# Coefficients of the next pair ahead of the high half of the weight three chunks on, in the output phase of a PEER block

## The chip, the cores and the metric

The kernel runs on one core of a Trainium2 chip. The metric is the device time of one execution in microseconds (us); several executions of one build are given by their median. A core has a matrix engine (TensorE, PE in the profile, with its weight loads as PEld), VectorE (DVE), ScalarE (ACT), GpSimd (POOL) and SyncE (SP). Each engine works through its own queue of instructions in order. Here SyncE issues the large transfers and GpSimd the gathers.

## What is computed

One layer of a streaming encoder for 512 tokens of width 1024: a mixer (a gated convolution beside a gated recurrence), and then PEER, a retrieval over 16384 single-neuron experts. Only PEER matters here:

```python
best_s, best_pos = lax.top_k(cand_s, PEER_TOPK)      # 8 heads, 16 of 16384 experts each
idx = jnp.take_along_axis(cand_i, best_pos, axis=-1)
g = jax.nn.softmax(best_s, axis=-1)
u_sel = expert_u[idx]
act = jax.nn.gelu(jnp.einsum('phkd,pd->phk', u_sel, xb), approximate=False)
coef = (g * act.astype(jnp.float32)).astype(xb.dtype)
return jnp.einsum('phk,phkd->pd', coef, expert_v[idx])
```

All arrays are float32.

## The kernel before

**Two ways for PEER.** The first 128 tokens, and some of the work for 64 more, go the sparse way: GpSimd gathers the chosen rows of `u` and later of `v` (`gath`, L747), and VectorE does one step of some 1.2 us for each gathered tile of 128 rows: a dot product (`dots`, L764) or a weighted sum (`sums`, L780). The other tokens go the dense way: TensorE multiplies with all experts, 128 of them in a chunk, and zero gates remove those that were not chosen.

**Chunks and jobs.** There are 128 `u` chunks (activations, line L87 to L89) and 128 `v` chunks (outputs, L1017). `jobs` (L797) lists them: 124 `u` chunks, then `v` and `u` alternately until the `u` chunks are done, then `v` alone. The first loop (L951, k below `CE` = 124) does the `u` chunks and the searches, the second (L1034) is the output phase.

**The weight's way.** Chunk k's weight is 512 KB. `w_load` (L806) has SyncE load it into `wraw` (4 buffers); `w_high` (L812) has ScalarE copy it to `whi`, rounded to the matrix engine's float32r (L73, 4 buffers); `w_low` (L816) has VectorE subtract, which leaves the rest in `wlo` (L78, 4 buffers). TensorE multiplies with both, so `whi` and `wlo` come free when TensorE is through with the chunk, and `wraw` when ScalarE and VectorE have read it. In round k the kernel asks for the load of chunk k+5, the high half of k+3 and the low half of k+2.

**The coefficients.** For a pair q of `v` chunks (2q and 2q+1), the coefficients are activations times gates. `v_gated(q)` (L896) has ScalarE copy 64 columns of the gates into `cf` (L901), VectorE multiply the other 640 (L903), and ScalarE round `cf` to `ch` (L907). `v_rest(q)` (L910) has VectorE subtract to get `cl` (L914). `cf` has one buffer, `ch` and `cl` two. A `v` chunk is 18 matmuls: for each of 3 token blocks two with `ch` and `whi`, two with `ch` and `wlo`, two with `cl` and `whi`. The first that needs `cl` is the fifth.

**The order around the change.** Both loops are written under a manual schedule: every engine gets its instructions in the order of the program text. A round of the output phase with an even `v` chunk n = 2q puts `w_high(k+3)` first, then `w_low(k+2)`, the gate loads (`v_gates`, L873, SyncE), the reload of spilled activations (`v_act`, L889, SyncE), `v_gated(q+1)`, the 18 matmuls, and a share of the sparse steps, one to three of them (L1058). An odd round has `v_rest(q+1)` in place of `v_gated`. `u_evict` (L833) is ScalarE's pass over a finished `u` chunk; the first matmuls of the output phase reuse the PSUM banks that it frees. The last two rounds of the first loop (k = 122 and 123) hold `v_gated(0)` and `v_rest(0)` for the first pair.

Of the kernel before, what the change touches and what calls it, by code (L numbers as in the profile page):

```python
# [34 lines left out]
def block_kernel(ctx, tc, xT, small, w_ada1, w_ada, b_ada, w_in, w_r, w_i, w_out, w_q, keys, uT, u, v, final_g, out):  # L35
# [35 lines left out]
    def high(raw):  # L71
        hi = wring.tile([128, KB, 128], FR, name="whi", bufs=WB)
        nc.scalar.activation(hi, raw, AF.Copy)  # L73
        return hi
# [10 lines left out]
    def mm3(ps, hi, lo, xh, xl, ks, first, last):  # L85
        for k in ks:
            nc.tensor.matmul(ps, hi[:, k, :], xh(k), start=first and k == ks[0], stop=False)  # L87
            nc.tensor.matmul(ps, hi[:, k, :], xl(k), start=False, stop=False)  # L88
            nc.tensor.matmul(ps, lo[:, k, :], xh(k), start=False, stop=last and k == ks[-1])  # L89
# [657 lines left out]
    def gath(table, idxs, k, key):  # L747
        if key not in rows:
            r = row_tile()
            nc.gpsimd.indirect_dma_start(out=r[:, :], out_offset=None, in_=table,  # L750
                                         in_offset=bass.IndirectOffsetOnAxis(ap=idxs[:, k:k + 1], axis=0))
            rows[key] = r
# [53 lines left out]
    def w_load(k):  # L806
        if k < len(jobs):
            kind, i = jobs[k]
            wraw[k] = load_w(uT[i] if kind == "u" else
                             v[vorder[i] * 128:(vorder[i] + 1) * 128, :].rearrange("p (k e) -> p k e", k=KB))  # L810

    def w_high(k):  # L812
        if k < len(jobs):
            whi[k] = high(wraw[k])

    def w_low(k):  # L816
        if k < len(jobs):
            wlo[k] = low(wraw.pop(k), whi[k])

    def weights(k):  # L820
        w_load(k + 5)
        w_low(k + 2)
# [4 lines left out]
    def spill(q):  # L827
        nc.sync.dma_start(Ad[q], act[q].rearrange("p c t -> p (c t)"))
        act[q] = None
# [3 lines left out]
    def u_evict():  # L833
        if unread:
            c, ps = unread.pop()
            if c % 2 == 0:
                act[c // 2] = ring.tile([128, 2, NU], F32, name="act", bufs=RB // 2)
            nc.scalar.activation(act[c // 2][:, c % 2], ps, AF.Gelu)  # L838

    def u_chunk(k, pool):  # L840
        c = jobs[k][1]
        ps = pool.tile([128, NU], F32, name="ps_act", bufs=2)
        mm3(ps, whi.pop(k), wlo.pop(k), hd, ld, range(KB), True, True)
        u_evict()
        unread.append((c, ps))
        q = c // 2 - RB // 2 + 2
        if c % 2 == 0 and 0 <= q < v0 // 2:
            spill(q)
        pe[0] += 3530
        dve[0] += 1140  # L850
        ac[0] += 1400
# [21 lines left out]
    def v_gates(n):  # L873
        if n >= NE or n in gdone:
            return
        gdone.add(n)
        cc = vorder[n]
        if n < 16 and n % 8 == 0:
            gt = gt8[:, n // 8]
            for t in (2, 3, 1):  # L880
                nc.sync.dma_start(gt[:, 8 * t - 8:8 * t], Gd[t][:, :, cc:cc + 8, :].rearrange("g j i t -> j g i t"))
            for k in range(0, 8, 2):
                gbuf[n + k] = gt[:, :, k:k + 2, :]
        for t in range(1, NT):
            m = n + (4 - t if n < 16 else 13 - 3 * t)
            if m >= 16 and m % 16 == 0 and m < NE:
                load_g16(m, t)

    def v_act(q):  # L889
        if q < NE // 2:  # L890
            c = vorder[2 * q] // 2
            if act[c] is None:
                act[c] = ring.tile([128, 2, NU], F32, name="act", bufs=RB // 2)
                nc.sync.dma_start(act[c].rearrange("p c t -> p (c t)"), Ad[c])
# [15 lines left out]
    def v_rest(q):  # L910
        if q < NE // 2:
            cf, ch = coef[q]
            cl = vp.tile([128, 2, ND], FR, name="cl", bufs=2)
            nc.vector.tensor_sub(cl, cf, ch.bitcast(F32))  # L914
            coef[q] = (ch, cl)
# [10 lines left out]
    def turn(k):  # L926

        awake = [g for g in "gsrd" if g in gens and asleep[g] <= k]
        if gopen and "g" in gens:
            gt = 96 * (k + 1 - gopen[0]) / (KD - KG - gopen[0])  # L930
            if "g" in awake and given["g"] < gt and ac[0] < pe[0] + AD:
                return "g"
            if "s" in awake and (given["g"] < gt and ac[0] < pe[0] + AD or given["s"] < NS * (k - gopen[0]) / (KD - gopen[0])):
                return "s"
        elif "s" in awake:
            return "s"
        elif "r" in awake and ("d" not in awake or given["d"] >= DS * (k - first[0])):
            return "r"
        for g in "dsg" if ac[0] < pe[0] + AD else "ds":
            if g in awake:  # L940
                return g
# [9 lines left out]
    for k in range(CE):  # L951
        weights(k)
        u_chunk(k, psE)
        cur[0] = k
        if sready and not first:
            first.append(k + 4)
            asleep["d"] = k + 4
            for m in range(GB_E - 1):
                gath(u, usteps[m][0], usteps[m][3], m)
        ac[0] = max(ac[0], pe[0] - LEAD)  # L960
        dve[0] = max(dve[0], RHO * pe[0] - LEAD - (HEAD if k < 9 else 0))
        xd = 0
        while dve[0] < RHO * pe[0] or k == KD:
            g = turn(k)
            if k == KD:
                g = next((g for g in "sg" if g in gens), None)
                if "s" not in gens and len(bdone) < XB:
                    g = "d"
            if g is None or (g == "d" and "g" not in gens and xd >= XD):
                break  # L970
            n = next(gens[g], 0)
            if n == 0:
                assert g != "d"
                late_k[g] = k
                del gens[g]
                continue
            if n is None:
                asleep[g] = k + 1
                continue
            dve[0] += n  # L980
            xd += g == "d"
            if gopen or g == "d":
                given[g] += 1 if g in "gd" else n
        w_high(k + 3)
        if k == KD:
            ep.close()
            vp = ctx.enter_context(tc.tile_pool(name="vp", bufs=2, reuse_waits="tile"))
            gp = ctx.enter_context(tc.tile_pool(name="gp", bufs=1, reuse_waits="tile"))
            late[:] = [gp, taken[0] + 10]
            gt8 = vp.tile([128, 2, NG, 8, 16], F32, name="gt", bufs=1)  # L990
        m = k - CE + XE
        if 0 <= m < XE:
            for n in [0] if m < 2 else range(5) if m == XE - 1 else [8]:
                v_gates(n)
        if m >= XE - 2:
            (v_gated, v_rest)[m - XE + 2](0)
    u_evict()
    psx.close()

# [12 lines left out]
    def v_chunk(n, b):  # L1012
        hi, lo, ch, cl = vsp[n]
        bs = slice(b * 128, (b + 1) * 128)
        for st, mv, first, last in ((ch, hi, n == 0, False), (ch, lo, False, False), (cl, hi, False, n == NE - 1)):
            for e in range(2):
                nc.tensor.matmul(accs[b][e], st[:, bs], mv[:, e * 512:(e + 1) * 512], start=first, stop=last)  # L1017
# [15 lines left out]
    steps, done = len(usteps) - len(bdone) + 128, 0  # L1033
    for k in range(CE, len(jobs)):  # L1034
        w_load(k + 5)
        w_high(k + 3)
        w_low(k + 2)
        kind, n = jobs[k]
        if kind == "u":
            u_chunk(k, psP)  # L1040
        else:
            q, e = divmod(n, 2)
            v_gates(n + 5)
            if e == 0:
                v_act(q + 4)
                v_gated(q + 1)
            else:
                v_rest(q + 1)
            vsp[n] = [w.pop(k).rearrange("p k e -> p (k e)") for w in (whi, wlo)] + [c[:, e] for c in coef[q]]
            if n < NE - VT:  # L1050
                for b in range(3):
                    v_chunk(n, b)
                del vsp[n]
            u_evict()
            pe[0] += 4090
            dve[0] += 2005
        if kind == "v":
            share = min((n + 1) / (NE - VE), 1) * (steps + 0.31 * (NE - RB)) - 0.31 * max(n + 1 - RB, 0)  # L1058
            while done < share and next(sparse, None):
                done += 1  # L1060
# [53 lines left out]
CE = 124  # L1114
# [56 lines left out]
```

## Time and profile before

| | |
|---|---|
| median of 3 runs | 1396.99 us (1394.65 to 1399.21) |
| profiled execution | 1397.99 us, of which the span is 1396.2 us |
| TensorE busy | 1343.5 us, 96% |
| VectorE busy | 1243.7 us, 89% |
| ScalarE busy | 757.2 us, 54% |
| GpSimd busy | 531.2 us, 38% |
| transfers | 440.07 MB, mean 315 GB/s; 413 to 414 GB/s from 1100 to 1250 us |
| output phase | first `v` matmul at 831.6 us, last of its loop at about 1371 us |

The profile is of one execution. Its views are: busy time by engine in stretches of the span (with the granted TensorE clock as a fraction), groups of instructions, who waited for whom, and the timeline of one engine. In a timeline row the columns are start in us, duration in us, engine, line of the kernel, operation, result and operands, shapes and count; a bracket at the end gives the idle time ahead of the row and what ended it. Successive rows overlap a little, since an instruction's recorded duration includes the tail of its writes.

### The profile page before, as it was taken

The page shows a single profiled execution, that of the slowest core. Times are in us where ns is not written, and L with a number is a line of the kernel's source. Part 1 is how long each engine was busy: PE and PEld are TensorE (multiplying, and loading weights), DVE is VectorE, ACT ScalarE, POOL GpSimd, SP SyncE. Part 2 cuts the span into 40 slices and gives each one's busy share as a digit, 9 for nine tenths or more (in the row PEclk, how much of TensorE's full clock was granted, in tenths as well). Part 3 has the DMA queues.
Part 4 walks back from the last instruction along what each step waited for, and adds up shares of the span by engine and source line. Part 5 has one row for each costly group of instructions (what it writes and reads, how often), then busy time and mean ns, then how long its engine had stood idle before and what let it go on. Part 6 is the DMA issues. An engine that isn't in the chain of part 4 may idle for free.

```text
span 1396.2 us, 21690 instructions
## 1 busy us (share of the span) xinstructions
PE 1343.5 (96%) x7571; PEld 1167.7 (84%) x7571; DVE 1243.7 (89%) x2452; ACT 757.2 (54%) x1237; POOL 531.2 (38%) x334
## 2 busy tenths in 40 slices
PE   5999998999999999999999989999999999999996
PEld 2566786789999999999999988877778888888885
DVE  6687766899999999999999967898989898898998
ACT  3576634435598699856995434333333433343443
POOL 0000000000245244414342435666756676665660
PEclk9999998999999999999999999999999999999998
DMA  8676332234789999979999999999999999999994
GB/s 350 236 279 210 126 100 81 76 93 143 242 312 387 316 352 373 384 217 347 355 372 340 329 388 376 385 372 414 401 414 409 415 411 415 413 415 412 407 364 178
DMA packets 146929, 440.07 MB, mean 315 GB/s; under 512 B 14722, under 2 KB 42370, under 8 KB 144772
## 3 DMA queue, kind: packets, MB, share of 16 engines
q1 hardware_dynamic: 99812, 267.75, 52.0%
q0 software_dynamic: 46720, 169.89, 31.6%
q8 instruction: 59, 0.97, 0.3%
q10 hardware_dynamic: 288, 1.05, 0.2%
q14 instruction: 50, 0.41, 0.1%
HBM read 393.54 MB, written 45.09 MB: 314 GB/s over the span
## 4 chain that ended last, share of the span: by engine, by line
PE 66%; DVE 15%; DMA 8%; issue 6%; ACT 4%; DVEq 0%; SPq 0%; ACTq 0%
PE acc L1017 26%; PE ps_act L87 7%; PE ps_act L88 7%; PE ps_act L89 7%; DMA wraw<-in_v_dram 6%; PE ps_gt L642 4%; PE ps_z L89 4%; PE ps_z L88 4%; PE ps_z L87 4%; DVE wlo L78 3%; DVE scr L771 3%; DMA rows<-in_u_dram,idx_s 1%; DVE igh L636 1%; ACT whi L73 1%; DVE jh L626 1%
## 5 line engine op out<-in xcount | busy, mean ns | idle before, releaser
L73 ACT ACTIVATE whi<-wraw 128x1024 fp32r<-128x1024 f32 x292 | 308.6, 1057 | 377.6 <-DMA wraw<-in_v_dram 148.4
L78 DVE TENSOR_TENSOR wlo<-wraw,whi 128x1024 fp32r<-128x1024 f32 x292 | 355.6, 1219 | 67.5 <-ACT whi L73 59.5
L87 PE MATMUL ps_act<-h,whi 128*128 128x320 f32 x1024 | 322.4, 315 | 1.6 <-ACT sc L515 1.2
L88 PE MATMUL ps_act<-h,whi 128*128 128x320 f32 x1024 | 317.1, 310 | 0.0
L89 PE MATMUL ps_act<-h,wlo 128*128 128x320 f32 x1024 | 316.9, 309 | 0.0
L750 POOL DMA_INDIRECT rows<-in_u_dram,idx_s x128 | 202.3, 1580 | 225.8 <-DVE scr L771 185.2
L750 POOL DMA_INDIRECT rows<-in_v_dram,idx_s x128 | 226.0, 1766 | 117.7 <-DVE ys L787 90.4
L1017 PE MATMUL acc<-whi,ch 128*128 128x512 f32 x750 | 233.1, 392 | 7.6 <-ACT act L838 4.7
L1017 PE MATMUL acc<-whi,cl 128*128 128x512 f32 x750 | 233.2, 392 | 4.2 <-DVE cl L914 4.2
L1017 PE MATMUL acc<-wlo,ch 128*128 128x512 f32 x750 | 232.2, 391 | 0.0
L87 PEld LDWEIGHTS ps_act<-h,whi 128*128 128x128 f32 x1024 | 193.1, 189 | 2.2 <-ACT sc L515 1.4
L88 PEld LDWEIGHTS ps_act<-h,whi 128*128 128x128 f32 x1024 | 193.0, 189 | 0.2
L89 PEld LDWEIGHTS ps_act<-h,wlo 128*128 128x128 f32 x1024 | 192.8, 188 | 0.0
L750 POOL DMA_INDIRECT rows<-in_u_dram,idx_b x64 | 97.8, 1528 | 213.4 <-DVE scr L771 111.6
L1017 PEld LDWEIGHTS acc<-whi,ch 128*128 128x128 f32 x750 | 141.4, 189 | 38.3 <-ACT act L838 5.5
L1017 PEld LDWEIGHTS acc<-whi,cl 128*128 128x128 f32 x750 | 140.7, 189 | 36.8 <-DVE cl L914 7.7
L1017 PEld LDWEIGHTS acc<-wlo,ch 128*128 128x128 f32 x750 | 141.6, 189 | 29.6
L771 DVE SCALAR_TENSOR_TENSOR scr<-rows,h2n 128x1024 f16<-128x1024 f32 x128 | 156.2, 1220 | 9.8 <-DMA rows<-in_u_dram,idx_s 8.3
L787 DVE SCALAR_TENSOR_TENSOR ys<-rows,acts,ys 128x1024 f32<-128x1024 f32 x127 | 162.6, 1280 | 1.6
L838 ACT ACTIVATE act<-ps_act 128x320 f32<-128x320 f32 x128 | 55.5, 433 | 99.4 <-PE ps_act L89 95.4
L427 POOL DMA_DIRECT2D x1d<-xn x8 | 4.6, 570 | 270.2 <-ACT xn L426 270.2
L642 PE MATMUL ps_gt<-igh,jh 128*128 128x128 f32 x768 | 97.3, 275 | 2.8 <-DVE igh L636 1.3
(269 smaller groups left out, 1896.8 us busy)
## 6 DMA issues: line engine op xcount, KB each, us to landing
wraw<-in_uT_dram SPq DMA_DIRECT2D x128, 512.0 KB
wraw<-in_v_dram SPq DMA_DIRECT2D x128, 512.0 KB
Gd<-stg SPq DMA_DIRECT2D x46, 512.0 KB
wada<-in_w_ada_dram SPq DMA_DIRECT2D x16, 1024.0 KB
Ad<-act SPq DMA_DIRECT2D x48, 320.0 KB
act<-Ad SPq DMA_DIRECT2D x48, 320.0 KB
h<-Gd SPq DMA_DIRECT2D x12, 1024.0 KB
wraw<-in_w_in_dram SPq DMA_DIRECT2D x20, 512.0 KB
```

The costliest lines, as they stand in the source:

```text
L73: nc.scalar.activation(hi, raw, AF.Copy)
L78: nc.vector.tensor_sub(lo, raw, hi.bitcast(F32))
L87: nc.tensor.matmul(ps, hi[:, k, :], xh(k), start=first and k == ks[0], stop=False)
L88: nc.tensor.matmul(ps, hi[:, k, :], xl(k), start=False, stop=False)
L89: nc.tensor.matmul(ps, lo[:, k, :], xh(k), start=False, stop=last and k == ks[-1])
L626: nc.vector.tensor_tensor(jh, iota[:, None, :].to_broadcast([128, 4, 128]), sl[:, 1, t0:t0 + 4, None].to_broadcast([128, 4, 128]), op=OP.i ...
L642: nc.tensor.matmul(pg[:, :, k], jh[:, k, :], ig[:, k, :], start=True, stop=True)
L750: nc.gpsimd.indirect_dma_start(out=r[:, :], out_offset=None, in_=table, in_offset=bass.IndirectOffsetOnAxis(ap=idxs[:, k:k + 1], axis=0))
L771: nc.vector.scalar_tensor_tensor(scr, rows.pop(n), 1.0, hn, op0=OP.mult, op1=OP.mult, accum_out=dst[:, k:k + 1])
L787: nc.vector.scalar_tensor_tensor(ys, rows.pop(k), acts[:, k:k + 1], ys, op0=OP.mult, op1=OP.add)
L838: nc.scalar.activation(act[c // 2][:, c % 2], ps, AF.Gelu)
L1017: nc.tensor.matmul(accs[b][e], st[:, bs], mv[:, e * 512:(e + 1) * 512], start=first, stop=last)
```

## The change

In the rounds k = 122 and 123 of the first loop, and in each `v` round of the output phase, the call of `w_high(k + 3)` is moved behind the call of `v_gated` or `v_rest`. In a `u` round it stays ahead of the chunk's matmuls, now behind `w_low(k + 2)`.

```diff
@@ -981,7 +981,8 @@
             xd += g == "d"
             if gopen or g == "d":
                 given[g] += 1 if g in "gd" else n
-        w_high(k + 3)
+        if k < CE - 2:
+            w_high(k + 3)
         if k == KD:
             ep.close()
             vp = ctx.enter_context(tc.tile_pool(name="vp", bufs=2, reuse_waits="tile"))
@@ -994,6 +995,7 @@
                 v_gates(n)
         if m >= XE - 2:
             (v_gated, v_rest)[m - XE + 2](0)
+            w_high(k + 3)
     u_evict()
     psx.close()
 
@@ -1033,10 +1035,10 @@
     steps, done = len(usteps) - len(bdone) + 128, 0
     for k in range(CE, len(jobs)):
         w_load(k + 5)
-        w_high(k + 3)
         w_low(k + 2)
         kind, n = jobs[k]
         if kind == "u":
+            w_high(k + 3)
             u_chunk(k, psP)
         else:
             q, e = divmod(n, 2)
@@ -1046,6 +1048,7 @@
                 v_gated(q + 1)
             else:
                 v_rest(q + 1)
+            w_high(k + 3)
             vsp[n] = [w.pop(k).rearrange("p k e -> p (k e)") for w in (whi, wlo)] + [c[:, e] for c in coef[q]]
             if n < NE - VT:
                 for b in range(3):
```

## The prediction

> **What bounds the kernel now.** I read the page first. TensorE is the busiest engine, so I went to busy time by stretches, and then to the waits of two stretches of the output phase.
>
> ```profile
> span 1396.2 us, 21690 instructions
> 1050.00:1100.00 50.00, 50.00 (x222) 41.38 (x222) 45.93 (x45) 18.30 (x23) 31.11 (x19) 1.00 1.04 410
> ```
>
> From about 1050 to 1350 us TensorE has no gap (50.00 of 50.00). 222 matmuls in 50 us are 0.225 us each, 4.05 us for a chunk of 18 and 8.11 us for a pair. VectorE has 45.93 us of work in the same 50, and the transfer engines are full (share 1.04, 410 GB/s). So three resources stand close together, and whoever has to wait longer soon shows.
>
> ```profile
> ACT whi L73 <- PE acc L1017: 94.7, 41, 3.0
> ...
> ACT whi L73 <- DMA wraw<-in_v_dram: 76.4, 31, 7.5
> DVE wlo L78 <- ACT whi L73: 16.1, 5, 4.8
> ```
>
> These are the waits of 1050 to 1350 us (total, times, longest). TensorE is not among the waiting. ScalarE waits for a buffer or for the weight to land; VectorE's wait for the high half is 16.1 us in 5 events, each at a late weight. That is all the slack that VectorE has in 300 us.
>
> From 820 to 1050 us TensorE does wait, and these are the waits that the change could touch:
>
> ```profile
> ACT whi L73 <- DMA wraw<-in_v_dram: 72.0, 26, 8.3
> ...
> PEld acc L1017 <- DVE cl L914: 7.7, 9, 1.9
> PEld acc L1017 <- ACT act L838: 5.5, 2, 4.1
> ```
>
> **The change part by part.** Nothing is added or taken away. `w_high` is one ScalarE instruction, and only ScalarE's order changes: VectorE has no instruction of `w_high`, and `v_rest` none on ScalarE. SyncE's and GpSimd's orders stay. What is left is 64 places where ScalarE now does `cf` and `ch` of the next pair ahead of `whi` of chunk k+3. So `ch` no longer stands behind a weight that has not landed; in exchange `whi` stands behind VectorE's `cf` multiply, for which `ch` waits. Behind `whi`, VectorE's `wlo` of k+3 waits, and behind that in VectorE's queue stands `cl` of the very same pair.
>
> *The start of the phase.* Rows of VectorE, ScalarE and the weight loads:
>
> ```profile
> 827.45 0.82 DVE L903 TENSOR_TENSOR cf<-act,gt 128x640 f32<-128x640 f32 x1 [4.86 <-DMA gt<-Gd]
> 830.22 1.23 DVE L78 TENSOR_TENSOR wlo<-wraw,whi 128x1024 fp32r<-128x1024 f32 x1 [1.94 <-ACT whi L73]
> ```
> ```profile
> 829.13 1.06 ACT L73 ACTIVATE whi<-wraw 128x1024 fp32r<-128x1024 f32 x1 [7.87 <-DMA wraw<-in_uT_dram]
> ...
> 830.42 0.84 ACT L907 ACTIVATE ch<-cf 128x768 fp32r<-128x768 f32 x1
> 831.17 0.42 ACT L838 ACTIVATE act<-ps_act 128x320 f32<-128x320 f32 x1
> 831.90 1.06 ACT L73 ACTIVATE whi<-wraw 128x1024 fp32r<-128x1024 f32 x1 [0.31 <-DMA wraw<-in_v_dram]
> ```
> ```profile
> 831.64 0.29 PEld L1017 LDWEIGHTS acc<-whi,ch 128*128 128x128 f32 x1 [4.08 <-ACT act L838]
> 833.33 0.29 PEld L1017 LDWEIGHTS acc<-whi,ch 128*128 128x128 f32 x1 [1.41 <-ACT act L838]
> ```
>
> Now `cf` and `ch` fit into ScalarE's wait for the weight, and the eviction at 831.17 moves to about 830.1: TensorE's first wait shrinks from 4.08 to 3.0 us. But the second eviction stands behind the `whi` at 831.90, which waits for its own weight as before. TensorE reaches that point 1.07 us earlier and waits 1.07 us longer. Term: 0. If that weight were not late, 1.07 us would be gained.
>
> *The price of the new order in a steady pair.* VectorE rows, then ScalarE rows, of one pair:
>
> ```profile
> 1319.39 0.82 DVE L903 TENSOR_TENSOR cf<-act,h 128x640 f32<-128x640 f32 x1
> ...
> 1321.32 1.22 DVE L78 TENSOR_TENSOR wlo<-wraw,whi 128x1024 fp32r<-128x1024 f32 x1
> 1322.46 0.95 DVE L914 TENSOR_TENSOR cl<-cf,ch 128x768 fp32r<-128x768 f32 x1
> ...
> 1326.97 0.81 DVE L903 TENSOR_TENSOR cf<-act,h 128x640 f32<-128x640 f32 x1
> ```
> ```profile
> 1317.93 1.06 ACT L73 ACTIVATE whi<-wraw 128x1024 fp32r<-128x1024 f32 x1 [3.01 <-PE acc L1017]
> ...
> 1320.30 0.85 ACT L907 ACTIVATE ch<-cf 128x768 fp32r<-128x768 f32 x1 [1.11 <-DVE cf L903]
> ```
>
> From `cf`'s start to `ch`'s start are 0.91 us (1319.39 to 1320.30), from `ch` to ScalarE's next instruction 0.75 (830.42 to 831.17), from `whi` to the `wlo` that waits for it 1.09 (829.13 to 830.22). So in the new order `wlo` of k+3 starts no earlier than 2.75 us after `cf`. In this pair one sparse step stands between, and before `wlo` came 1.93 us after `cf`: VectorE would idle for 0.82 us. With two steps between, the cover holds:
>
> ```profile
> 1365.05 0.82 DVE L903 TENSOR_TENSOR cf<-act,h 128x640 f32<-128x640 f32 x1
> ...
> 1368.30 1.22 DVE L78 TENSOR_TENSOR wlo<-wraw,whi 128x1024 fp32r<-128x1024 f32 x1
> ```
>
> 3.25 us against 2.75: nothing, as long as TensorE or the weight doesn't hold `whi` up. In VectorE's timeline 26 of the 64 pairs have one step there. The first of them is
>
> ```profile
> 873.04 0.82 DVE L903 TENSOR_TENSOR cf<-act,gt 128x640 f32<-128x640 f32 x1
> ```
>
> and the last the one at 1326.97 above. Three are before 1000 us, 8 from 1006 to 1064, 8 from 1138 to 1195, 7 from 1276 to 1327. In such a pair VectorE's round grows from 7.58 us (1319.39 to 1326.97) to 8.40, beyond TensorE's 8.11: instead of gaining 0.53 us it loses 0.29. Between 1050 and 1350 there are 17 of them, 13.9 us, against the 16.1 us that VectorE waited there anyway: it just fits, if the late weights land when they did. VectorE's lead covers a run: TensorE starts the chunks of this pair some 8.11 us after 1317.93, at 1326.0, and wants `cl` after four matmuls, at 1326.9; `cl` is done at 1323.4. A lead of 3.5 us against 8 x 0.29 = 2.3 for a run. After a late weight the lead is smaller, so I put 0.2 us a run, 0.6 in all (my estimate; 0 if the lead always holds, 2.3 a run if there is none).
>
> *Where TensorE waits for coefficients.* The two `ch` waits look like the gain:
>
> ```profile
> 969.44 0.30 PEld L1017 LDWEIGHTS acc<-whi,ch 128*128 128x128 f32 x2 [1.64 <-ACT ch L907]
> 970.49 0.30 PEld L1017 LDWEIGHTS acc<-whi,cl 128*128 128x128 f32 x2 [0.29 <-DVE cl L914]
> ...
> 1029.74 0.30 PEld L1017 LDWEIGHTS acc<-whi,ch 128*128 128x128 f32 x2 [2.08 <-ACT ch L907]
> 1031.33 0.32 PEld L1017 LDWEIGHTS acc<-whi,cl 128*128 128x128 f32 x2 [0.83 <-DVE cl L914]
> ```
> ```profile
> 967.25 1.06 ACT L73 ACTIVATE whi<-wraw 128x1024 fp32r<-128x1024 f32 x1 [8.04 <-DMA wraw<-in_v_dram]
> ```
> ```profile
> 968.35 1.22 DVE L78 TENSOR_TENSOR wlo<-wraw,whi 128x1024 fp32r<-128x1024 f32 x1 [2.30 <-issue]
> 969.49 0.95 DVE L914 TENSOR_TENSOR cl<-cf,ch 128x768 fp32r<-128x768 f32 x1
> ```
>
> At 969 the `ch` wait (1.64 us) goes: `ch` is done long before the weight lands. But `cl` is next: it stands on VectorE behind `wlo` (968.35), which starts 1.1 us after the `whi` at 967.25, whose weight lands as late as ever. TensorE starts 1.64 us earlier, does four matmuls, and waits until 970.49 as before. Term: 0. At 1029 it is worse:
>
> ```profile
> 1027.31 0.82 DVE L903 TENSOR_TENSOR cf<-act,gt 128x640 f32<-128x640 f32 x1
> ...
> 1030.33 0.95 DVE L914 TENSOR_TENSOR cl<-cf,ch 128x768 fp32r<-128x768 f32 x1
> ```
>
> This is a pair with one step, and `cl` at 1030.33 is what TensorE waits for: it comes 0.82 us later. Term: +0.8. The other `cl` waits (7.7 us in 9) follow a weight late for `wlo` of k+2, which the change doesn't move, with two steps behind `cf`: 0.
>
> *The end.* The last moved `whi`:
>
> ```profile
> 1366.89 1.06 ACT L73 ACTIVATE whi<-wraw 128x1024 fp32r<-128x1024 f32 x1 [3.01 <-PE acc L1017]
> ```
>
> Its buffer and that of the last `ch` are given back by the same matmul, at 1366.89. With `ch` first, `whi` starts 0.75 us later and `wlo` at 1368.74 instead of 1368.30; VectorE is on the chain that ends last from there on. Term: at most +0.4.
>
> Sum: 0 + 0.8 + 0 + 0.6 + 0.4 = 1.8, say +2 us on the profiled execution: 1397.99 to 1400. The median of the runs shown lies 1.0 below the profiled time, so I say 1399.
>
> **Rivals.** *VectorE becomes the bound (slower).* The fit above assumes that late weights land when they did. A load is issued only when `wlo` of four chunks earlier has freed its buffer, so VectorE's delay can come back as a later weight.
>
> ```profile
> 1279.78 9.29 SPq L68 DMA_DIRECT2D wraw<-in_v_dram  x1
> ```
>
> For it: SyncE's loads wait mostly for `wlo`. Against: this late weight was held 9.29 us in its issue with the transfer engines full, so a backlog set its time, and a slower VectorE also asks for fewer gathers. If the delay comes back whole, the 23 one-step pairs from 1006 us cost 23 x 0.82 = 18.9, less a lead of 3.5: +15 us, 1412. If half of it comes back, 9.5 - 3.5: +6. It decides from the point where a run of one-step pairs eats more than the 3.5 us.
>
> *The waits really go (faster).* If `cl` came earlier too and the second eviction did, 1.07 + 1.64 + 2.08 = 4.8 us would be gained. There is the clock as well:
>
> ```profile
> 830.00:834.00 4.00, 1.46 (x3) 0.86 (x4) 3.78 (x5) 2.94 (x6) 1.14 (x1) 0.52 1.09 334
> 834.00:838.00 4.00, 4.00 (x13) 3.15 (x12) 3.70 (x6) 0.00 (x0) 1.52 (x2) 0.63 1.02 340
> ```
>
> Behind the wait of 4.08 us the granted clock (third number from the end) was 0.52 and 0.63: 0.48 x 4 + 0.37 x 4 = 3.4 us lost. If a first wait of 3.0 us kept the clock up, 3.4 us would come back, and with the waits 8.2: 1389. Against: a second wait, then 2.5 us, follows at once, so TensorE idles as much in all, and `cl`'s queue argues against the rest.
>
> The Trainium skill ("TensorE: Matmul & The Clock Gate", Part 1) says that the clock halves after a window of about 3.4 us without work; 3.0 us would then be short enough, and the sum would be 1.8 - 3.4 = -1.6. The trace agrees with the halving (0.52), and its row doesn't show where the threshold is.
>
> *It does nothing.* All of it hidden: 0, 1397.
>
> **How the numbers follow.** Forecast 0.52, VectorE the bound 0.33, waits gone 0.11, nothing 0.04. A measurement of this kernel can tell about 0.3%, 4.2 us, from no change: 1392.8 to 1401.2. Same: the forecast, the nothing, and 0.02 of the rivals, 0.58. Slower: most of the first rival and none of the forecast, 0.32. Faster: most of the second, 0.10. The range goes from 1394, part of the way to the faster case, to 1410, most of the way to the slower one; that leaves out about 2 in 10.
>
> **What would show it.** Right: `whi` waits for nothing after `ch` in even rounds; VectorE's waits for `whi` change from 5 long ones to many of about 0.8 us in one-step pairs; TensorE's `ch` waits are gone and its `cl` waits are as long or longer; the first `act` wait is near 3.0 us and the second near 2.5. Wrong: `cl` waits that shrink, a clock near 1.00 at 830 to 838 us, or TensorE with gaps after 1050.

## The result, and the profile after

The changed kernel takes 1407.01 us (median of 6 runs, 1402.53 to 1409.37) against 1397.86 us (6 runs, 1394.65 to 1399.21): a ratio of 1.0068, with a 95% interval of 1.0052 to 1.0083. That is 9.2 us slower, on the side of the first rival and not of the forecast.

The profiled execution is the fastest of the six: 1402.53 us, with a mean granted clock of 0.990 where the other five have 0.985 to 0.987. Its span is 4.6 us longer than that of before, half of the median's loss; the clock rows below bear on the other half. The span, and the engines' shares of the chain that ended last:

```profile
span 1400.8 us, 21714 instructions
...
DVE 28%; issue 26%; PE 21%; DMA 14%; POOL 6%; ACT 4%; DVEq 0%; SPq 0%; ACTq 0%; POOLq 0%
```

The same row of before:

```profile
PE 66%; DVE 15%; DMA 8%; issue 6%; ACT 4%; DVEq 0%; SPq 0%; ACTq 0%
```

Before, one piece of the chain was TensorE's matmuls without a break, from 1031 to 1363 us:

```profile
1031.33 331.46 PE acc L1017 x1454
```

After, VectorE has the largest share: the chain has moved from TensorE to VectorE. The steady part, 1050 to 1350 us, by busy time of each engine (first number: the stretch; then TensorE with its count of matmuls), of after and of before:

```profile
1050.00:1350.00 300.00, 298.52 (x1302) 242.91 (x1301) 278.79 (x257) 113.40 (x147) 179.71 (x112) 1.00 1.02 401
```
```profile
1050.00:1350.00 300.00, 300.00 (x1325) 248.39 (x1325) 282.29 (x263) 116.05 (x146) 200.21 (x114) 1.00 1.03 410
```

23 matmuls fewer in the same 300 us, at 0.225 us each 5.2 us. TensorE now has gaps where it had none. The waits of after from 1050 to 1355 us (total, times, longest):

```profile
ACT ch L907 <- DVE cf L903: 119.2, 35, 4.1
...
ACT whi L73 <- DMA wraw<-in_v_dram: 27.6, 15, 4.7
DVE wlo L78 <- ACT whi L73: 19.8, 23, 1.7
PEld acc L1019 <- DVE cl L914: 7.0, 15, 0.9
```

ScalarE's time in front of a late weight (76.4 us before) has become time in front of VectorE's multiply (119.2 us), and that costs nothing by itself. What costs is the third row: VectorE waited 5 times, up to 4.8 us, 16.1 in all, and now waits 23 times, 1.7 at most, 19.8 in all. Of these 23, 18 lie in the one-step pairs of this stretch. The fourth row had no counterpart before. One pair shows the chain, first on VectorE, then on ScalarE:

```profile
1313.98 0.82 DVE L903 TENSOR_TENSOR cf<-act,h 128x640 f32<-128x640 f32 x1
1314.72 1.28 DVE L787 SCALAR_TENSOR_TENSOR ys<-rows,acts,ys 128x1024 f32<-128x1024 f32 x1
1316.74 1.23 DVE L78 TENSOR_TENSOR wlo<-wraw,whi 128x1024 fp32r<-128x1024 f32 x1 [0.75 <-ACT whi L73]
...
1322.41 0.82 DVE L903 TENSOR_TENSOR cf<-act,h 128x640 f32<-128x640 f32 x1
```
```profile
1314.91 0.85 ACT L907 ACTIVATE ch<-cf 128x768 fp32r<-128x768 f32 x1 [4.10 <-DVE cf L903]
1315.67 1.99 ACT L73 ACTIVATE whi<-wraw 128x1024 fp32r<-128x1024 f32 x2
```

`ch` starts 0.93 us after the multiply, `whi` 0.76 later, `wlo` 1.07 after that: 2.76 us from multiply to `wlo` (2.75 was worked out). The multiply and one sparse step fill 2.0 of them, and VectorE idles 0.75. Its round is 1322.41 - 1313.98 = 8.43 us. TensorE's pair is shorter; in before, where it had no gap, these two rows stand six rows of `cl` loads, which is one pair, apart:

```profile
1318.41 0.41 PEld L1017 LDWEIGHTS acc<-whi,cl 128*128 128x128 f32 x2
...
1326.58 0.41 PEld L1017 LDWEIGHTS acc<-whi,cl 128*128 128x128 f32 x2
```

That is 8.17 us, and 8.16 on average from 1297 to 1344 us; the prediction had 8.11 from a count of matmuls in 50 us. In after, TensorE falls into VectorE's step, by its weight loads:

```profile
1318.89 0.30 PEld L1019 LDWEIGHTS acc<-whi,cl 128*128 128x128 f32 x2 [0.39 <-DVE cl L914]
1327.31 0.30 PEld L1019 LDWEIGHTS acc<-whi,cl 128*128 128x128 f32 x2 [0.40 <-DVE cl L914]
1335.74 0.30 PEld L1019 LDWEIGHTS acc<-whi,cl 128*128 128x128 f32 x2 [0.39 <-DVE cl L914]
1344.64 0.30 PEld L1019 LDWEIGHTS acc<-whi,cl 128*128 128x128 f32 x2 [0.85 <-DVE cl L914]
```

The first three are 8.42 us apart, with a wait of 0.4 in each. The fourth belongs to a pair with two steps, in which `cl` comes later behind the multiply. There is no `ch` wait any more.

### The profile page after: what moved, and what is told of

It reads as the page before. It is cut to its first block, busy times and chain, and to the rows that moved or that the text cites. A ratio compares the mean times of both kernels' runs of the same rounds, so it can differ in the third digit from the quotient of the medians.

```text
span 1400.8 us, 21714 instructions
## 1 busy us (share of the span) xinstructions
PE 1344.2 (96%) x7571; PEld 1163.4 (83%) x7571; DVE 1245.2 (89%) x2452; ACT 752.5 (54%) x1237; POOL 508.6 (36%) x334
## 4 chain that ended last, share of the span: by engine, by line
DVE 28%; issue 26%; PE 21%; DMA 14%; POOL 6%; ACT 4%; DVEq 0%; SPq 0%; ACTq 0%; POOLq 0%
DMA wraw<-in_v_dram 8%; PE acc L1019 8%; POOL rows L750 6%; DVE wlo L78 5%; DVE scr L771 4%; PE ps_z L89 3%; PE ps_z L87 3%; PE ps_z L88 3%; DMA rows<-in_u_dram,idx_s 3%; DVE cl L914 3%; DVE cf L903 2%; ACT whi L73 2%; DVE ys L787 2%; DMA rows<-in_u_dram,idx_b 2%; DVE rep L476 1%
## 5 line engine op out<-in xcount | busy, mean ns | idle before, releaser
L73 ACT ACTIVATE whi<-wraw 128x1024 fp32r<-128x1024 f32 x292 | 303.7, 1051 | 151.1 <-PE ps_z L88 59.1
L750 POOL DMA_INDIRECT rows<-in_v_dram,idx_s x128 | 205.1, 1602 | 143.2 <-DVE ys L787 115.0
L907 ACT ACTIVATE ch<-cf 128x768 fp32r<-128x768 f32 x64 | 54.3, 848 | 204.2 <-DVE cf L903 200.3
```

The costliest lines, as they stand in the source:

```text
L907: nc.scalar.activation(ch, cf, AF.Copy)
```

## The experiments

The theory after the result: in pairs with one sparse step behind the multiply, `wlo` of chunk k+3 waits for a `whi` that stands behind `ch`, VectorE idles 0.75 us, its round is longer than TensorE's, and TensorE waits for `cl`. Rivals: the loss comes from the start of the phase; from the single `cf` buffer, for which ScalarE's copy now waits; from the order on ScalarE or the loads as such, whatever VectorE does. All runs were timed against the kernel before on the same chip.

**Only the part in the first loop.** The output phase is that of before; rounds 122 and 123 are changed.

Against the changed kernel:

```diff
         w_load(k + 5)
+        w_high(k + 3)
         w_low(k + 2)
         kind, n = jobs[k]
         if kind == "u":
-            w_high(k + 3)
...
                 v_rest(q + 1)
-            w_high(k + 3)
```

> Only the part of the change in the first loop (rounds 122 and 123) is kept; the output phase has the high half in front again. Theory (VectorE's wlo of chunk k+3 waits for whi, which now waits for ch and the multiply, and idles about 0.8 us in pairs with one sparse step between): no such pair is touched, so the time is that of the kernel before, within 2 us. Rival (the start: the first output matmuls and the clock after them): the whole +9 us stays.

1397.78 us against 1397.75, ratio 0.9997 (0.9986 to 1.0008). The start has no part in the loss.

**`whi` between the copy and `ch`.**

```diff
             nc.scalar.activation(cf[:, :, 0:XB].rearrange("p c (g t) -> p c g t", t=16),
...
+            if kh is not None:
+                w_high(kh)
             ch = vp.tile([128, 2, ND], FR, name="ch", bufs=2)
...
-                v_gated(q + 1)
+                v_gated(q + 1, k + 3)
             else:
                 v_rest(q + 1)
-            w_high(k + 3)
+                w_high(k + 3)
```

> In even rounds of the output phase ScalarE's order is cf copy, whi of k+3, ch. The copy still stands in front of whi and still waits for the single cf buffer (for cl of the pair before), but whi no longer stands behind the multiply. Theory: the 0.8 us idles of VectorE go, time as before, within 3 us. Rival (the single cf buffer holds ScalarE up): stays at +6 to +9 us.

1397.19 us against 1397.75, ratio 1.0004 (0.9994 to 1.0015): the loss is gone. VectorE's rows of one pair in this run, and its wait from 1050 to 1355 us:

```profile
1317.17 0.82 DVE L903 TENSOR_TENSOR cf<-act,h 128x640 f32<-128x640 f32 x1
...
1319.10 1.22 DVE L78 TENSOR_TENSOR wlo<-wraw,whi 128x1024 fp32r<-128x1024 f32 x1
```
```profile
DVE wlo L78 <- ACT whi L73: 16.1, 6, 4.3
```

`wlo` again comes 1.93 us after the multiply, with no wait, and the 16.1 us are back in a few long ones. The copy into `cf` still stood ahead of `whi`, so the single buffer is not it. The harm is in standing behind `ch`, and through it behind the multiply.

**The dose.** The sparse steps are dealt out otherwise; the order is the changed one.

```diff
-            while done < share and next(sparse, None):
+            while done < share + 0.6 * (n % 2 == 0) and next(sparse, None):
```

> The changed kernel with the sparse steps dealt out otherwise: the target of even rounds is 0.6 step higher, so that two or more stand between the multiply and wlo; their number in all stays. Theory: 3.2 us of cover against 2.75 us, the idles go, time within 3 us of before. Rival (a late wlo is not the cause, but later weights or the order as such): stays at +6 to +9 us.

1398.13 us against 1397.75, ratio 1.0000 (0.9990 to 1.0009). The other way:

```diff
-            while done < share and next(sparse, None):
+            while done < share - 0.5 * (n % 2 == 0) and next(sparse, None):
```

> The opposite: the target of even rounds is 0.5 step lower, so that nearly every pair after the first 30 chunks has one step there. Theory: VectorE's round is 8.40 us against 8.11 in some 45 pairs instead of 23, with no stretch to recover the lead: +13 to +20 us against before. Rivals: +9 us as with the change alone.

1415.66 us against 1397.75, ratio 1.0132 (1.0118 to 1.0147): +18 us. Its waits from 1050 to 1355 us:

```profile
DVE wlo L78 <- ACT whi L73: 24.5, 33, 0.8
PEld acc L1019 <- DVE cl L914: 14.9, 35, 1.7
...
ACT whi L73 <- DMA wraw<-in_v_dram: 1.5, 3, 1.2
```

Every wait of VectorE for `whi` is now a short one, and TensorE waits in nearly every pair. ScalarE hardly waits for a late weight any more (1.5 us against 76.4 before), so later loads are not what costs here. Counted on VectorE's timeline from 1000 us on:

| run | pairs with one step behind the multiply | ratio to before |
|---|---|---|
| two steps in even rounds | 0 | 1.0000 |
| the change | 23 | 1.0068 |
| one step in even rounds | 45 | 1.0132 |

Some 0.4 us for each such pair, in both: 9.2 / 23 and 18.5 / 45 (0.0132 of 1397.75 is 18.5). That is an average over all pairs, not the price of each. The idle is 0.75 us, but VectorE's round without it is 7.59, 0.57 shorter than TensorE's pair, and VectorE had waited for late weights anyway: 16.1 us in long waits before, against 24.5 us in short ones with one step in even rounds. Part of the idle only takes the place of those waits.

**The control.** The dealing with one step in even rounds, in the order of before.

> Control for the run with one step in even rounds: the kernel before (high half in front) with the same dealing of the sparse steps. Theory: the number of steps between the multiply and wlo costs nothing by itself, only whi behind ch makes it matter: time as before, within 4 us. Rival (the uneven dealing delays VectorE or the gathers by itself): +8 us or more, and the dose run would have to be read against this.

1397.66 us against 1397.16, ratio 1.0000 (0.9987 to 1.0013). The dealing costs nothing by itself; it takes the changed order to make it matter.

**The cost by itself.** Order of before; a multiply that nobody reads in even rounds with one step.

```diff
+            had = done
             while done < share and next(sparse, None):
                 done += 1
+            if n % 2 == 0 and done - had == 1:
+                pad = rowp.tile([128, D], F16, name="scr")
+                nc.vector.tensor_mul(pad[:, 0:640], h2n[:, 0:640], h2n[:, 0:640])
```

> The disputed cost by itself: the order of the kernel before, and in each even round with one sparse step VectorE does one more multiply of 640 columns that nobody reads, some 0.7 us, about as long as it idled there. The instructions of ScalarE are those of before. Theory (it is VectorE's round beyond TensorE's 8.11 us, whatever fills it): +6 to +11 us. Rival (the later whi and ch on ScalarE, or the loads behind them, cost by themselves): 0 to +3 us.

1409.07 us against 1396.56, ratio 1.0094 (1.0077 to 1.0111): +13 us, above the range that the theory gave, and far from the rival's. Rows of VectorE:

```profile
1317.80 0.82 DVE L903 TENSOR_TENSOR cf<-act,h 128x640 f32<-128x640 f32 x1
...
1319.73 0.82 DVE L1064 TENSOR_TENSOR scr<-h2n 128x640 f16<-128x640 f32 x1
...
1326.12 0.82 DVE L903 TENSOR_TENSOR cf<-act,h 128x640 f32<-128x640 f32 x1
```

The round is 8.32 us, again longer than TensorE's pair, and TensorE's waits for `cl` from 1050 to 1355 us are 9.2 us in 20, with ScalarE's instructions as they were. More time in VectorE's round alone is enough for a loss of this size. That the run loses more than the change is not established, since the two intervals overlap (1.0083 and 1.0077).

**VectorE's order.** With the changed order on ScalarE, the coefficients were put ahead of `wlo` of k+2 on VectorE too:

```diff
-        w_low(k + 2)
         kind, n = jobs[k]
         if kind == "u":
+            w_low(k + 2)
             w_high(k + 3)
...
                 v_rest(q + 1)
+            w_low(k + 2)
             w_high(k + 3)
```

> The changed order on ScalarE, and on VectorE too the coefficients in front: the multiply (even rounds) and cl (odd rounds) stand ahead of wlo of k+2. Between the multiply and wlo of k+3 now lie wlo of k+2, a step and cl, 3.9 us against 2.75 us. Theory: no idle, the loss of 9 us is gone; cl no longer stands behind wlo, so the waits of TensorE for cl after late weights shrink as well: 1392 to 1398 us. Rival (high half behind ch is harmful as such): +6 to +9 us.

1397.62 us against 1397.16, ratio 0.9997 (0.9983 to 1.0011). The loss is gone, as expected; the hoped-for gain is not there. And the same order on VectorE with ScalarE as before:

```diff
         w_high(k + 3)
-        w_low(k + 2)
         kind, n = jobs[k]
         if kind == "u":
+            w_low(k + 2)
             u_chunk(k, psP)
...
                 v_rest(q + 1)
+            w_low(k + 2)
```

> The kernel before with VectorE's order alone changed: multiply and cl ahead of wlo of k+2, ScalarE as before (high half first). Theory: TensorE's cl waits before 1031 us shrink where a late weight had held wlo and with it cl, but ch is behind the late high half again: between the run with both and the kernel before, 1394 to 1398 us. Rival (VectorE's throughput sets cl in that stretch, not the order): as before within 1 us.

1406.74 us against 1397.16, ratio 1.0067 (1.0044 to 1.0090): 9 us slower, where a gain or nothing was expected, a miss. Its waits from 1050 to 1355 us:

```profile
PEld acc L1017 <- ACT ch L907: 7.4, 6, 2.1
DVE cl L914 <- ACT ch L907: 6.9, 7, 1.9
```

Here TensorE waits for `ch`. One place, on ScalarE and by the weight loads:

```profile
1296.92 1.06 ACT L73 ACTIVATE whi<-wraw 128x1024 fp32r<-128x1024 f32 x1 [1.12 <-DMA wraw<-in_v_dram]
...
1298.21 0.84 ACT L907 ACTIVATE ch<-cf 128x768 fp32r<-128x768 f32 x1
```
```profile
1299.10 0.30 PEld L1017 LDWEIGHTS acc<-whi,ch 128*128 128x128 f32 x2 [1.55 <-ACT ch L907]
```

`ch` stands behind a `whi` whose weight was late, and `cl` and TensorE wait for it. The two runs differ in ScalarE's order alone, so with this order on VectorE, coefficients first on ScalarE is worth about 9 us. That `wlo`, moved back in its round, makes the loads later and the late weights worse would explain why this run suffers where the kernel before doesn't. ScalarE's waits for late weights fit it, 114.0 us here against 76.4 before, but the cause isn't shown by that: they are 104.8 us in the control, which loses nothing. A fifth load buffer, which would test it, was not tried.

**The multiply alone ahead of `wlo`,** in even rounds:

```diff
-        w_low(k + 2)
         kind, n = jobs[k]
+        if kind == "u" or n % 2:
+            w_low(k + 2)
...
                 v_gated(q + 1)
+                w_low(k + 2)
```

> The changed order on ScalarE; on VectorE only the multiply of even rounds is moved ahead of wlo of k+2, cl stays behind wlo of k+3. Between the multiply and wlo of k+3 lie wlo of k+2 and at least one step: 1.93 + 1.14 = 3.1 us against 2.75. Theory: no idle, time as before within 3 us, or a few us better, as wlo of odd rounds and with it the next load is not later than before. Rival (with the coefficients ahead of wlo on VectorE each load comes later and costs): +4 us or more.

1395.80 us against 1397.46, ratio 0.9993 (0.9980 to 1.0005). The loss is gone here too; whether there is a small gain can't be told.

**The steps dealt out more evenly over the chunks,** in the order of before and in that of the last run:

```diff
-            share = min((n + 1) / (NE - VE), 1) * (steps + 0.31 * (NE - RB)) - 0.31 * max(n + 1 - RB, 0)
+            share = min((n + 1) / (NE - VE), 1) * (steps + 0.1 * (NE - RB)) - 0.1 * max(n + 1 - RB, 0)
```

> The kernel before with the sparse steps dealt out more evenly over the chunks (0.1 instead of 0.31 step fewer in each chunk past the 32nd). If VectorE's round of 8.7 us with four steps a pair, against 8.11 for TensorE, is what makes TensorE wait for cl between 916 and 988 us, those waits (about 6 us) go: 1390 to 1395 us. If the late weights alone make them: no change.

> The order of the run with the multiply first in even rounds, with the steps dealt out more evenly (0.1 instead of 0.31). Theory: both effects add, the waits for cl before 988 us go and ch is not held by late weights: 1387 to 1394 us, better than either kernel. If VectorE's lead is too small later on, where a pair then has a little more work: 1395 to 1400 us.

1397.98 us (ratio 1.0006, 0.9995 to 1.0017) and 1397.21 us (1.0001, 0.9989 to 1.0014), both against 1397.46: no gain; in both the lesser of the two cases named beforehand came. In the first of them TensorE's `cl` waits, from 820 to 1050 us and from 1050 us to the end, were:

```profile
PEld acc L1017 <- DVE cl L914: 4.9, 3, 2.5
```
```profile
PEld acc L1017 <- DVE cl L914: 3.7, 5, 1.8
```

7.7 us before 1050 and none after it in the kernel before; 4.9 and 3.7 here. The waits have moved, and their sum has not shrunk. None of the versions beats the kernel before by more than its runs scatter.

## Why the prediction was right and wrong

The range (1394 to 1410) holds 1407.0; the likeliest case (about 1399, no change that can be measured) did not come, and the first rival, VectorE as the bound, did. It had been given 0.33. The range held because it was drawn to take in most of that rival, not because the sum was right. Of the signs that I had named for being wrong, one came: TensorE with gaps after 1050 us.

**Right: the order and its price.** ScalarE is the only engine whose order changed, the cover was 2.76 us against 2.75 worked out, the idle 0.75 against 0.82, the round 8.43 against 8.40 (TensorE's pair 8.16 against 8.11), and the one-step pairs from 1000 us on are the 23 that were counted. The two-step pairs cost nothing, as the run with two steps everywhere shows.

**Right: the start.** ScalarE's rows of after, and the weight loads:

```profile
829.91 0.42 ACT L838 ACTIVATE act<-ps_act 128x320 f32<-128x320 f32 x1
831.74 1.06 ACT L73 ACTIVATE whi<-wraw 128x1024 fp32r<-128x1024 f32 x1 [1.41 <-DMA wraw<-in_v_dram]
```
```profile
830.38 0.19 PEld L1019 LDWEIGHTS acc<-whi,ch 128*128 128x128 f32 x1 [4.47 <-ACT act L838]
833.17 0.28 PEld L1019 LDWEIGHTS acc<-whi,ch 128*128 128x128 f32 x1 [2.60 <-ACT act L838]
```

The first eviction came at 829.91 (830.1 was worked out), and the second still waited for its late weight: TensorE's second wait is 2.60 us (2.5), and at 833.17 it stands where it stood at 833.33. The first wait did not shrink to 3.0, since in this execution TensorE was done earlier, at 825.91 instead of 827.56.

**Wrong: the lead.** The step that failed is "A lead of 3.5 us against 8 x 0.29 = 2.3 for a run", and with it the 0.2 us a run. The 3.5 us were read from a pair late in its run, where the lead has been built up. Behind the late weight at the head of that run it is small in before too. These are `cl` four pairs earlier, and the weight load that uses it, four pairs ahead of the one at 1326.58:

```profile
1292.11 0.95 DVE L914 TENSOR_TENSOR cl<-cf,ch 128x768 fp32r<-128x768 f32 x1
```
```profile
1293.93 0.41 PEld L1017 LDWEIGHTS acc<-whi,cl 128*128 128x128 f32 x2
```

`cl` is done at 1293.06, a lead of 0.9 us. In before it grows from there with each pair; in after the longer rounds of a run of one-step pairs keep it from doing so. TensorE's `cl` waits from 1050 us on are 7.0 us in 15, and by the count of matmuls it lost 5.2 us: some 1.7 for each of the three runs, not 0.2, and near the 2.3 that I had named for no lead. So 13.9 us of idle in a slack of 16.1 did not "just fit". The rival's half-way case said +6, the whole +15, and +9.2 lies between.

**Wrong: the end.** I gave it at most 0.4 us. VectorE's last two multiplies in after, and TensorE's last wait:

```profile
1362.01 0.82 DVE L903 TENSOR_TENSOR cf<-act,h 128x640 f32<-128x640 f32 x1
...
1369.60 0.82 DVE L903 TENSOR_TENSOR cf<-act,h 128x640 f32<-128x640 f32 x1
```
```profile
1374.98 0.19 PEld L1012 LDWEIGHTS acc<-whi,cl 128*128 128x128 f32 x1 [1.66 <-DVE cl L914]
```

The last multiply is at 1369.60 instead of 1365.05, 7.59 us after the one ahead of it, VectorE's own pace without an idle. It arrives 4.55 us late, and the span is 4.6 us longer: the end is VectorE's backlog, not the order of the last `whi`. In the profiled execution this backlog arises late. The multiply behind VectorE's last long wait in before, and the same pair's multiply in after:

```profile
1289.05 0.82 DVE L903 TENSOR_TENSOR cf<-act,gt 128x640 f32<-128x640 f32 x1
```
```profile
1288.47 0.82 DVE L903 TENSOR_TENSOR cf<-act,gt 128x640 f32<-128x640 f32 x1
```

Up to here nothing of the one-step pairs shows in VectorE's time: after stands 0.58 us ahead. (In the run with one step in even rounds the same multiply is 8.1 us late, at 1297.17, so there the earlier pairs did cost.) From here to the last multiply, ten rounds with six one-step pairs, before takes 76.00 us and after 81.13. In before the ten rounds are 7.58 to 7.74 us each, so VectorE had no long wait left to take the idles in, and they went to the end whole. TensorE's lead is not what counts there: VectorE's own work runs on to the end of the span.

**Incomplete: the other `cl` waits.** I had put all nine before 1050 us down to late weights. Four of them, 0.63 to 0.68 us each, come where VectorE takes 8.70 us from one `cl` to the next, in pairs with four steps and no late weight. The term of 0 does not change by it.

**Where the profiled execution and the median differ.** The same four microseconds in after and in before, the granted clock third from the end:

```profile
1030.00:1034.00 4.00, 4.00 (x19) 3.29 (x18) 3.97 (x7) 0.47 (x1) 3.15 (x2) 1.00 1.04 417
```
```profile
1030.00:1034.00 4.00, 3.61 (x11) 2.49 (x11) 3.96 (x7) 1.06 (x1) 2.53 (x2) 0.69 1.06 418
```

In before, waits of 2.08 and 0.83 us stood ahead of this place and the clock fell to 0.69; in the profiled execution of after, TensorE waited

```profile
1029.19 0.30 PEld L1019 LDWEIGHTS acc<-whi,cl 128*128 128x128 f32 x2 [1.40 <-DVE cl L914]
```

once, and the clock stayed at 1.00. So the term of +0.8 at 1029 did not show here; this execution came through that place some 2 us earlier. The five others have the lower mean clock and no trace, so that this is what sets them apart is argued and not shown.

**The clock rule.** The Trainium skill ("TensorE: Matmul & The Clock Gate", Part 1) would have let a first wait of 3.0 us pass. It could not be put to the test, as that wait was 4.47 us; the clock behind it fell again:

```profile
830.00:834.00 4.00, 1.37 (x3) 0.92 (x4) 3.96 (x5) 2.02 (x5) 1.32 (x1) 0.59 1.01 308
```

0.59, near the half that the page names, so the trace agrees with it there. The fall to 0.69 in before, behind two waits that are each below 3.4 us, shows that the length of a single wait doesn't settle it.

**The second rival** (the waits go) was right in one thing: `ch` waits vanish. As worked out, `cl` takes their place.

## What to carry to other kernels

Moving an instruction ahead of another on one engine makes the second inherit every wait of the first; follow what then stands behind the second on a third engine, and compare that engine's round with the round of the bound, not its mean load over the phase. A lead is worth what it is after the worst event, not what it is in a quiet place, and an idle behind the last wait that could have taken it in goes to the end whole. And where a step's cover varies from round to round, count the rounds with the thin cover: their number gave the loss here, on average 0.4 us each at 0, 23 and 45.

## What the runs showed that I had not expected

The order "coefficients first" on ScalarE costs about 9 us with one order on VectorE (the change) and saves about 9 us with another (the two runs with `wlo` last). Neither order of ScalarE is better by itself.
